# Inverse square roots of the second group's norms computed on DVE instead of POOL

## The chip, the cores and the metric

The kernel runs on one core of a Trainium2 chip. The metric is the device time of one execution in microseconds (us), the median of several runs. In the text, PE is the matrix engine (TensorE), PEld its weight loads, DVE the vector engine, ACT the scalar engine, POOL GpSimd and SP the engine that issues most DMAs.

## The reference, cut to what matters

A block of layers maps `x` (512 tokens of 1024 numbers) to an output of the same shape: a Mamba-2 mixer, a sliding-window attention, a hybrid mixer (gated delta rule and mLSTM), a cross-attention to a memory of 256 tokens, and a feed-forward layer that picks 128 of 16384 experts per token (PEER). Between them stand RMS norms, and these are what the change touches:

```python
def rmsnorm(x, w):
    xf = x.astype(jnp.float32)
    y = xf * lax.rsqrt(jnp.mean(xf * xf, axis=-1, keepdims=True) + EPS)
    return (y * w.astype(jnp.float32)).astype(x.dtype)
```

Every layer norms its input; the Mamba and attention layers also norm their output (`post_norm`) and, inside, the gated outputs; the hybrid layer norms each head (128 numbers) separately; a final norm ends the kernel. In each case one number per token (or one per token and head) goes through `1/sqrt(mean + EPS)`.

## The kernel before, in words

The 512 tokens are four blocks of 128, each block on the 128 partitions. Two **groups** of two blocks go through the layers one after the other: `run` iterates over `GROUPS`, and for each group `layers` runs `mamba`, `swa`, `hybrid`, `cross` and `route`. The last group ends in `dense`, which multiplies by all 16384 experts instead of gathering some.

The first group's experts are fetched by **gathers**: 512 indirect DMAs on POOL's queue (`Rows.next`, L1955), each of 128 rows of 4 KB, and for each a **gather product** on DVE of 128x1024 elements (`Rows.take`, L1989 with the table `p_u`, L1995 with `p_v`). These run as side work while the second group goes through its layers: `after` is a generator that `run` advances by a share at each `yield` of `layers`. It first finishes the first group's routing, then sets `self.rows = Rows(...)` (L1928; until then `self.rows` is None) and places the gathers. `self.quiet` is a flag that stops `run` from advancing it, set by the last part of each output projection (`out_part`) and by the hybrid's `finish`, cleared at the end of the next `norm_T`. What is left of the gathers by the time of `dense` is placed there, in `steps`.

The order of the instructions on each engine is fixed when the program is built: a list scheduler takes, among the instructions that are ready in its own model, the one of highest priority, which is the program's order raised by `high_priority(HP)` in `norm_T` and `post` and lowered for the side work. Inside `manual_schedule` (in `dense`) the order is the one written. On the chip each engine runs its queue strictly in this order.

`rstd` (L457) makes the inverse square roots. `v = ss * scale + EPS` is one DVE instruction (L460), then one POOL instruction raises `v` to the power -0.5 (L462), reading a constant tile `mhalf`. Its callers are

- `norm_T` (L499, tile `nr`, 128x1): the sums of squares of a block, then `xn = x * r` in two DVE instructions (L502), then PE transposes (L414) of both blocks, eight ACT copies (L512) into `hh`, and the first matmuls of the next layer;
- `post` (L613, tile `pr`, 128x1), at the end of `mamba` and `swa`, once for each block, with the residual update L618 behind it;
- `mamba` (L851, tile `gr`, 128x2), the gate norm, read later by `post` (L612, L615);
- `finish` in `hybrid` (L1380, tile `or`, 128x4), four times for a group: both blocks for the mLSTM heads, then both for the delta-rule heads. L1378 and L1379 scale the sums before it, L1382 and L1383 apply the result, and a POOL instruction (L1381) multiplies by the gate;
- `final` (L1866, tile `finr`, 128x1), once for each block of the kernel, between an ACT square with its sum (L1865) and the DVE product L1871 with the weights that a DMA brings (`gu<-in_bcw`, L1869); then the output DMA (L1872). For the first group's two blocks `final` is a side work of `Rows` (`ends`), for the second group's it is the end of `dense`.

The weights come as DMAs on SP's queue; ACT and DVE split the unrounded ones into a high and a low part (L378, L381).

Of the kernel before, what the change touches and what calls it, by code (L numbers as in the profile page):

```python
# [9 lines left out]
F32 = mybir.dt.float32  # L10
F32R = mybir.dt.float32r
BF16 = mybir.dt.bfloat16
I32 = mybir.dt.int32
U32 = mybir.dt.uint32
AF = mybir.ActivationFunctionType
ALU = mybir.AluOpType
# [171 lines left out]
class Kern:  # L188
# [268 lines left out]
    def rstd(self, ss, n, name, scale):  # L457
        nc = self.nc
        v = self.pp.tile([128, n], F32, name=name + "v", tag="rsv", bufs=2)
        nc.vector.tensor_scalar(v, ss, scale, EPS, op0=ALU.mult, op1=ALU.add)  # L460
        r = self.pp.tile([128, n], F32, name=name + "r", tag="rsr", bufs=3)
        nc.gpsimd.tensor_tensor(r, v, self.mhalf[:, :n], op=ALU.pow)  # L462
        return r

    def hT_open(self, gt, halo, full):
        nc = self.nc
        hx = [self.hp.tile([128, 8, gt + 4], F32 if full else F32R, name=n, tag=n) for n in ("hh", "hl")[:1 if full else 2]]
        if full:
            hx.append(None)
        if halo is not None and full:  # L470
            nc.gpsimd.tensor_tensor(hx[0][:, :, 0:4], *[h.bitcast(F32) for h in halo[0]], op=ALU.add)
        elif halo is not None:
            for j in range(2):
                if halo[0] is None:
                    nc.vector.tensor_copy(hx[j][:, :, 0:4], self.zero[:, None, :].to_broadcast([128, 8, 4]))
                else:
                    nc.gpsimd.tensor_copy(hx[j][:, :, 0:4], halo[0][j])
        self.hx = hx
        self.hT_cur = [t if t is None else t[:, :, 4:] for t in hx]
        return self.hT_cur  # L480
# [1598 lines left out]
```

## Time and profile before

| what | value |
|---|---|
| median of 3 runs | 2506.41 us (2500.04 to 2513.98) |
| the profiled execution | 2507.27 us |
| its span, first to last instruction | 2505.5 us |
| PE busy | 2346.4 us, 94% of the span |
| DVE busy | 1975.4 us, 79% |
| ACT busy | 1177.5 us, 47% |
| POOL busy | 1075.9 us, 43% |
| mean granted clock of PE | 0.97 |

How to read it: a share of busy time is a mean over stages with different limits, and PE's counts pipelined matmuls. The second group's layers run from about 800 us to about 1600 us of the span, `dense` from there to the end. In a timeline row stand the start, the busy time, engine, line, operation, output and inputs, the shape, how many instructions were merged, and in brackets the engine's idle time before it with what released it.

### The profile page before, as it was taken

To read this page: it belongs to the slowest core of one execution; us is meant where nothing else is said; L and a number is where in the kernel's file an instruction comes from. 1 tells how busy PE (TensorE), PEld (TensorE's weight loads), DVE (VectorE), ACT (ScalarE), POOL (GpSimd) and SP (SyncE) were. 2 spreads that over 40 slices of the span, in tenths; PEclk is the share of its full clock that TensorE was granted. 3 is DMA by queue.
4 is the path that set the end of the run, shared out by engine and by line. 5 is a ranking of instruction groups with operands and counts; after the bars stand their busy time and mean duration, and the time that the engine had idled before them with its cause. 6 is when DMAs were issued, how large, how long until landed. Compare 5 with 4: busy or idle time off the path is not lost.

```text
span 2505.5 us, 40945 instructions
## 1 busy us (share of the span) xinstructions
PE 2346.4 (94%) x14872; PEld 2117.7 (85%) x14872; DVE 1975.4 (79%) x3978; ACT 1177.5 (47%) x2451; POOL 1075.9 (43%) x910
## 2 busy tenths in 40 slices
PE   7999998999988999989899968999999999999997
PEld 7999898998888888877778857888999999888864
DVE  7777666757579888877789775799888988888886
ACT  6766566744554433424343222226754454444433
POOL 1111101232010577764648664322246666666663
PEclk9999999999999999999989989999999999999999
DMA  6554434423545799977988768877989999899985
GB/s 205 180 173 158 163 98 142 130 93 103 172 136 166 287 379 363 377 275 277 358 326 297 258 197 329 282 241 239 302 290 355 347 366 360 321 357 344 340 295 176
DMA packets 203961, 642.32 MB, mean 256 GB/s; under 512 B 21104, under 2 KB 53360, under 8 KB 202480
## 3 DMA queue, kind: packets, MB, share of 16 engines
q1 hardware_dynamic: 97216, 347.19, 39.9%
q0 software_dynamic: 73728, 268.47, 29.6%
q10 hardware_dynamic: 32816, 24.06, 3.0%
q8 instruction: 117, 1.92, 0.3%
q14 instruction: 84, 0.69, 0.1%
HBM read 621.74 MB, written 17.89 MB: 255 GB/s over the span
## 4 chain that ended last, share of the span: by engine, by line
PE 63%; DVE 14%; DMA 8%; issue 7%; POOL 4%; ACT 4%; ACTq 0%; DVEq 0%; POOLq 0%; SPq 0%
PE mm L406 41%; PE ax L406 16%; DMA gu<-in_p_v,eid 4%; PE tp L414 3%; DVE wlo L381 3%; PE tp L406 3%; DVE x L1995 2%; POOL gu L1955 1%; DVE cacc L535 1%; ACT whi L378 1%; DMA gd<-gst 1%; DVE act L1811 1%; DMA ol<-in_p_v,eid 0%; DVE xn L502 0%; DVE wk L1531 0%
## 5 line engine op out<-in xcount | busy, mean ns | idle before, releaser
L381 DVE TENSOR_TENSOR wlo<-wraw,whi 128x1024 fp32r<-128x1024 f32 x285 | 353.0, 1244 | 124.0 <-ACT whi L378 122.0
L406 PE MATMUL mm<-hl,whi 128*128 128x256 f32 (+1 forms) x1376 | 391.8, 285 | 0.0
L378 ACT CAST whi<-wraw 128x1024 fp32r<-128x1024 f32 x285 | 298.0, 1050 | 125.8 <-PE mm L406 82.0
L1955 POOL DMA_INDIRECT gu<-in_p_u,eid x190 | 250.2, 1317 | 245.7 <-DVE gu L1989 162.0
L406 PE MATMUL mm<-hh,whi 128*128 128x260 f32 (+1 forms) x1232 | 331.5, 343 | 2.7 <-DVE spp L566 1.5
L1955 POOL DMA_INDIRECT gu<-in_p_v,eid x206 | 297.5, 1444 | 68.8 <-issue 33.1
L406 PE MATMUL mm<-hh,wlo 128*128 128x260 f32 (+1 forms) x1200 | 321.7, 340 | 4.0 <-DVE wlo L381 4.0
L1995 DVE SCALAR_TENSOR_TENSOR x<-gu,act,x 128x1024 f32<-128x1024 f32 x206 | 272.3, 1322 | 48.4 <-DMA gu<-in_p_v,eid 45.2
L406 PEld LDWEIGHTS mm<-hl,whi 128*128 128x128 f32 x1376 | 262.6, 191 | 5.0
L406 PEld LDWEIGHTS mm<-hh,whi 128*128 128x128 f32 x1232 | 235.2, 194 | 21.6 <-ACT hh L512 2.8
L1989 DVE SCALAR_TENSOR_TENSOR gu<-gu,hf 128x1024 f32<-128x1024 f32 x190 | 239.4, 1274 | 17.0 <-DMA gu<-in_p_u,eid 14.5
L406 PEld LDWEIGHTS mm<-hh,wlo 128*128 128x128 f32 x1200 | 231.7, 196 | 20.6 <-DVE wlo L381 4.8
L1818 POOL TENSOR_TENSOR w<-act,w 128x256 fp32r<-128x256 f32 x128 | 146.5, 1144 | 211.9 <-issue 158.7
L406 PE MATMUL mm<-dhh,wlo 128*128 128x256 f32 x752 | 211.6, 281 | 0.0
L406 PE MATMUL mm<-dhh,whi 128*128 128x256 f32 x752 | 209.8, 279 | 0.0
L1813 ACT CAST w<-act 128x256 fp32r<-128x256 f32 x128 | 52.2, 408 | 326.0 <-DVE act L1811 326.0
L406 PE MATMUL mm<-wlo,hh 128*128 128x256 f32 x656 | 175.5, 328 | 0.0
L406 PE MATMUL mm<-whi,hh 128*128 128x256 f32 x608 | 166.8, 328 | 0.4 <-ACT hh L512 0.4
L406 PE MATMUL mm<-whi,oh 128*128 128x256 f32 x560 | 147.0, 326 | 0.0
L406 PE MATMUL mm<-hh,wraw 128*128 128x256 f32 (+1 forms) x608 | 145.4, 385 | 0.4 <-ACT act L1713 0.4
L406 PEld LDWEIGHTS mm<-dhh,whi 128*128 128x128 f32 x752 | 141.1, 188 | 4.0
L406 PEld LDWEIGHTS mm<-dhh,wlo 128*128 128x128 f32 x752 | 141.2, 188 | 0.0
(504 smaller groups left out, 5913.6 us busy)
## 6 DMA issues: line engine op xcount, KB each, us to landing
wraw<-in_w SPq DMA_DIRECT2D x238, 512.0 KB
wraw<-in_p_v SPq DMA_DIRECT2D x78, 512.0 KB
wraw<-in_p_ut SPq DMA_DIRECT2D x69, 512.0 KB
whi<-in_w SPq DMA_DIRECT2D x55, 512.0 KB
wlo<-in_w SPq DMA_DIRECT2D x55, 512.0 KB
wrawd<-in_p_v SPq DMA_DIRECT2D x50, 512.0 KB
wrawd<-in_p_ut SPq DMA_DIRECT2D x36, 512.0 KB
gd<-gst ACTq DMA_DIRECT2D x32, 384.0 KB
```

What stands on the lines that cost most here:

```text
L378: nc.scalar.copy(hi, raw)
L381: (nc.gpsimd if le == "P" else nc.vector).tensor_tensor(lo, raw, hi.bitcast(F32), op=ALU.subtract)
L406: inst = self.last = self.nc.tensor.matmul(out, lhsT, rhs, start=start, stop=stop, skip_group_check=True)
L414: return self.nc.tensor.transpose(out, in_, self.ident[:in_.shape[0], :in_.shape[0]])
L535: nc.vector.scalar_tensor_tensor(acc, ps[:, 1 + j:1 + j + gt], w[:, j:j + 1], acc, op0=ALU.mult, op1=ALU.add)
L1811: nc.vector.tensor_tensor(act, act, G[:, e // 16 % 2, :, e % 16], op=ALU.mult)
L1813: nc.scalar.copy(wt[:, 0:gt], act)
L1818: nc.gpsimd.tensor_tensor(wt[:, gt:2 * gt], act, wt[:, 0:gt].bitcast(F32), op=ALU.subtract)
L1955: self.behind(k.nc.gpsimd.indirect_dma_start(out=t, out_offset=None, in_=table, in_offset=bass.IndirectOffsetOnAxis(ap=self.res[b][0][:, s ...
L1989: self.behind(nc.vector.scalar_tensor_tensor(t, t, 1.0, self.hf[:, b, :], op0=ALU.mult, op1=ALU.mult, accum_out=acts[b][:, s:s + 1]))
L1995: self.behind(nc.vector.scalar_tensor_tensor(x[:, b, :], t, acts[b][:, s:s + 1], x[:, b, :], op0=ALU.mult, op1=ALU.add))
```

## The change

`rstd` calls a new function `pow`. While `self.rows` is None it issues the POOL instruction as before. Later it issues 14 DVE instructions: the bits of `v` as an integer are shifted right by one and subtracted from a constant, which gives a first guess, and three Newton steps of four instructions each refine it, every instruction reading the result of an earlier one. One more small tile (`rst`) is allocated. Nothing else is changed.

```diff
@@ -459,8 +459,24 @@
         v = self.pp.tile([128, n], F32, name=name + "v", tag="rsv", bufs=2)
         nc.vector.tensor_scalar(v, ss, scale, EPS, op0=ALU.mult, op1=ALU.add)
         r = self.pp.tile([128, n], F32, name=name + "r", tag="rsr", bufs=3)
-        nc.gpsimd.tensor_tensor(r, v, self.mhalf[:, :n], op=ALU.pow)
+        self.pow(r, v, n)
         return r
+
+    def pow(self, r, v, n):
+
+        nc = self.nc
+        if self.rows is None:
+            nc.gpsimd.tensor_tensor(r, v, self.mhalf[:, :n], op=ALU.pow)
+            return
+        t = self.pp.tile([128, n], F32, name="rst", tag="rst", bufs=2)
+        ri = r.bitcast(I32)
+        nc.vector.tensor_scalar(ri, v.bitcast(I32), 1, None, op0=ALU.logical_shift_right)
+        nc.vector.tensor_scalar(ri, ri, -1.0, 1597463007.0, op0=ALU.mult, op1=ALU.add)
+        for _ in range(3):
+            nc.vector.tensor_tensor(t, r, r, op=ALU.mult)
+            nc.vector.tensor_tensor(t, t, v, op=ALU.mult)
+            nc.vector.tensor_scalar(t, t, -0.5, 1.5, op0=ALU.mult, op1=ALU.add)
+            nc.vector.tensor_tensor(r, r, t, op=ALU.mult)
```

## Rows read from the trace of the kernel before

**Rows 1.** Page, chain of waits that ended last: shares of the span by engine.
```profile
PE 63%; DVE 14%; DMA 8%; issue 7%; POOL 4%; ACT 4%; ACTq 0%; DVEq 0%; POOLq 0%; SPq 0%
```

**Rows 2.** Line L462, 800 to 1600 us: ns min/median/max, first and last start.
```profile
L462 POOL TENSOR_TENSOR nr<-nv,mhalf x8: 545/554/579, 1098.7 to 1590.2; 128x1 f32<-128x1 f32 x8
L462 POOL TENSOR_TENSOR pr<-pv,mhalf x4: 544/561/573, 1089.9 to 1246.9; 128x1 f32<-128x1 f32 x4
```

**Rows 3.** Timeline, Mamba's end to the attention's norm.
```profile
1097.50 0.19 ACT L493 ACTIVATION_READ_ACCUMULATOR xn<-x 128x1 f32 x1
...
1099.26 0.88 DVE L502 TENSOR_SCALAR xn<-x,nr 128x512 f32<-128x512 f32 x2 [1.94 <-POOL nr L462]
...
1100.06 0.15 DVE L495 TENSOR_TENSOR ns<-nss 128x1 f32<-128x1 f32 x1
1100.24 0.15 DVE L460 TENSOR_SCALAR nv<-ns 128x1 f32<-128x1 f32 x1
1100.48 0.55 POOL L462 TENSOR_TENSOR nr<-nv,mhalf 128x1 f32<-128x1 f32 x1 [1.25 <-DVE nv L460]
1101.06 0.88 DVE L502 TENSOR_SCALAR xn<-x,nr 128x512 f32<-128x512 f32 x2 [0.66 <-POOL nr L462]
```

**Rows 4.** Timeline, first and last of six dependent DVE instructions (rope angles).
```profile
1102.48 0.17 DVE L881 TENSOR_SCALAR rk<-ang 128x16 f32<-128x16 f32 x1
...
1103.52 0.18 DVE L885 TENSOR_SCALAR ang<-ang 128x16 f32<-128x16 f32 x1
```

**Rows 5.** Groups by line and shape, DVE: count, busy us, mean ns.
```profile
L876 DVE MEMSET inv<- 128x1 f32 x16 | 0.3, 59 | 0.0
```

**Rows 6.** Timeline, the attention's end to the hybrid's norm, second block.
```profile
1249.48 0.19 ACT L493 ACTIVATION_READ_ACCUMULATOR xn<-x 128x1 f32 x1
...
1250.75 0.16 DVE L495 TENSOR_TENSOR ns<-nss 128x1 f32<-128x1 f32 x1
```

**Rows 7.** Timeline, the hybrid's end to the cross-attention's norm, both blocks.
```profile
1505.39 0.27 DVE L460 TENSOR_SCALAR nv<-ns 128x1 f32<-128x1 f32 x2
1508.47 0.94 POOL L1955 DMA_INDIRECT gu<-in_p_u,eid  x1 [5.67 <-DMA out<-gu]
...
1510.05 1.68 DVE L502 TENSOR_SCALAR xn<-x,nr 128x512 f32<-128x512 f32 x4 [4.39 <-POOL nr L462]
```

**Rows 8.** Timeline, the routing's norm, second block.
```profile
1590.82 0.88 DVE L502 TENSOR_SCALAR xn<-x,nr 128x512 f32<-128x512 f32 x2 [0.73 <-POOL nr L462]
```

**Rows 9.** Timeline, the hybrid's head norms.
```profile
1458.66 1.47 DVE L1379 TENSOR_TENSOR so<-so,cf 128x4 f32<-128x4 f32 x1
...
1460.12 1.27 DVE L1995 SCALAR_TENSOR_TENSOR x<-hl,act,x 128x1024 f32<-128x1024 f32 x1
...
1461.32 0.16 DVE L460 TENSOR_SCALAR ov<-so 128x4 f32<-128x4 f32 x1
...
1462.27 2.80 POOL L1381 TENSOR_TENSOR mixed<-mixed,hgate 128x512 f32<-128x512 f32 x2
...
1467.31 0.16 DVE L1382 TENSOR_TENSOR cf<-cf,or 128x4 f32<-128x4 f32 x1 [2.85 <-POOL or L462]
...
1468.31 0.29 PEld L414 LDWEIGHTS tp<-ident,mixed 128*128 128x128 f32 x2 [13.13 <-DVE mixed L1383]
```

**Rows 10.** Timeline, dense stage, the final norm of the first group's second block.
```profile
2473.88 0.15 DVE L460 TENSOR_SCALAR finv<-fss 128x1 f32<-128x1 f32 x1 [1.60 <-ACT gu L1865]
...
2474.82 1.23 DVE L381 TENSOR_TENSOR wlod<-wraw,whid 128x1024 fp32r<-128x1024 f32 x1 [0.78 <-ACT whid L378]
...
2477.25 1.71 DVE L1871 SCALAR_TENSOR_TENSOR gu<-x,finr,gu 128x1024 f32<-128x1024 f32 x1 [0.70 <-DMA gu<-in_bcw]
```

**Rows 11.** Timeline, the end of the kernel.
```profile
2495.46 0.15 DVE L460 TENSOR_SCALAR finv<-fss 128x1 f32<-128x1 f32 x1
...
2496.66 0.15 DVE L460 TENSOR_SCALAR finv<-fss 128x1 f32<-128x1 f32 x1 [1.04 <-ACT gu L1865]
...
2499.80 1.28 DVE L1871 SCALAR_TENSOR_TENSOR gu<-x,finr,gu 128x1024 f32<-128x1024 f32 x1 [0.42 <-DMA gu<-in_bcw]
```

## The prediction

> **What bounds the kernel.** I read the chain of waits first: PE makes up 63% of it, POOL 4% [rows 1]. So PE sets the time, and the change matters only where PE stands still for a norm. Then I read the line of the POOL power instruction, which shows how often it runs in the second group and that one takes 0.55 us [rows 2]. Last I read the timeline around each of them. The reader is to see the same picture at each layer's end: PE is out of work, and a string of short instructions on DVE, POOL and ACT runs with nothing beside it. What is added to this string is added to the time.
>
> **What changes sides.** `self.rows` is set early in the second group's Mamba layer, after its input norm; so that norm stays on POOL, and 21 calls change: 1 `gr`, 4 `pr`, 8 `nr`, 4 `or`, 4 `finr`. POOL loses 21 instructions, DVE gains 21 x 14 = 294. No DMA moves; no tile of any size is added.
>
> **The price of one chain.** Today, from the start of `nv` on DVE to the start of `xn`, which reads POOL's result, it takes 1101.06 - 1100.24 = 0.82 us [rows 3]. After the change 14 dependent DVE instructions lie between. The trace has none on integers, so I bound the step by the nearest rows. Below: independent 128x1 memsets take 0.06 us each [rows 5]. Above: six dependent instructions on 128x16 start over 1.04 us, five steps of 0.21 us [rows 4]. Nearest is the pair of dependent 128x1 instructions, 0.18 us [rows 3]; I take 0.19. Then `nv` to `xn` takes 15 x 0.19 = 2.85 us, and one **passage** costs 2.85 - 0.82 = +2.0 us (bounds: 15 x 0.06 - 0.82 = +0.1 and 15 x 0.21 - 0.82 = +2.3). Two chains whose inputs are ready together can share these 2.85 us, since an instruction of the other chain fits into each gap. [...]
>
> **Part by part.**
> 1. `gr`: 0. Its reader comes at the layer's end, behind the other output columns; without that cover, one passage, +2.0.
> 2. Mamba to attention: +1.7. On the path lie the second block's `pr` and then its `nr`, two passages, +4.0. Something comes back: the sum of squares for the second `nr` was there at 1097.50 + 0.19 = 1097.7, but DVE took it up only at 1100.06, since in its queue it stands behind the first block's `xn`, which had waited 1.94 us for POOL [rows 3]. The first block's chain can run beside the second's `pr` chain and be done by then: -2.3. If it can't, the gain falls away: +4.0. The first block's `pr` is hidden while PE still works on the second block's columns.
> 3. Attention to hybrid: +2.9. Again two passages, +4.0, and the second block's sum waited from 1249.67 to 1250.75 [rows 6], -1.1. Without that gain +4.0.
> 4. Hybrid's head norms (`or`): -1.0. PE stands 13.13 us for them [rows 9]. The first block's value went from 1461.32 to 1467.31, 6.0 us, mostly in POOL's queue behind other work. A chain of 15 steps of 0.2 us would be done at 1464.3, -3.0. But DVE instructions with two inputs get stuck while POOL multiplies: L1379, 128x4, took 1.47 us where 0.15 is usual. If the chain is held until L1381 ends, 1462.27 + 2.80 = 1465.1, it is done at 1468.1, +0.8. The second block gains the 2.85 us that DVE idled before L1382. I take -1.0, between the two, because the second block ends the wait; bounds -5.9 (-3.0 and the whole 2.85) and +5.1 (four gather products of 1.27 us in the gaps, rival A). The other two `or` come while PE works on the first half of the projection: 0. [...]
> 5. Final norm of the first group's first block: 0. It is side work; if it delays the output DMA, it delays the gather that waited for that DMA [rows 7] by at most one passage, +2.0.
> 6. Hybrid to cross: -1.7. Both `nv` are ready at 1505.39, but POOL's queue stood behind a gather that waited 5.67 us for an output DMA, so `xn` started at 1510.05 [rows 7]. Two chains side by side end at about 1505.5 + 2.85 = 1508.3. One after the other, with 0.84 us of `xn` between, the second `xn` starts at 1505.5 + 2 x 2.85 + 0.84 = 1512.0 instead of 1510.9: +1.1.
> 7. Cross to routing: +2.0, one passage, of the second block [rows 8]; the first block's runs while PE finishes.
> 8. Final norm in the dense stage: +1.2. The order there is as written, so 14 instructions stand in front of the split L381: it starts at 2473.88 + 2.85 = 2476.7, not 2474.82. L1871 stands behind L381, so it starts at 2476.7 + 1.23 = 2477.9 at the earliest, not at 2477.25 (+0.7), and at most the whole shift of L381 later (+1.9) [rows 10]; I take the middle. ACT queues behind its output DMA, and PE behind ACT. Bounds 0 (PE has slack there) and 1.9.
> 9. The last two final norms: +1.0. The weights' DMA hides much: the last product starts at 2499.80 [rows 11]. With the chains side by side the second ends at 2496.66 + 2.85 = 2499.5, and if the first product stands in its middle, the last starts at about 2500.8. One chain after the other: 2495.46 + 2.85 + 1.28 + 2.85 = 2502.4, +2.6.
>
> Sum: 0 + 1.7 + 2.9 - 1.0 + 0 - 1.7 + 2.0 + 1.2 + 1.0 = +6.1 us. The profiled execution took 2507.27 us, so 2513.4; it lies 0.9 above the median of the runs, so I give **2512.5 us**. About 0.5%, 12.5 us, is what a measurement of this kernel can tell from no change; the forecast is no change.
>
> **Rivals.**
> A. *Gather products in the gaps of the chains* (slower). The order is fixed at build time, and a step that isn't ready lets lower work pass. The trace shows it: between L1379 and L460, which needs it, stands a product of 1.27 us [rows 9]. A 14-step chain has 14 such gaps. Place: the `or` chains, in part `gr` and the side work's final norm. Each product on the path costs 1.27 us; it decides from five on (6.1 + 6.4 = 12.5). With ten, +18.8: 2525 us. For it: rows 9. Against it: at the four layer ends `quiet` keeps new products out.
> B. *Short steps* (faster). If dependent steps start as quickly as the memsets, 0.06 us, a passage costs +0.1 instead of +2.0: parts 2 and 3 become -2.1 and -0.9, part 4 -5, part 6 -3.7, part 7 +0.1, parts 8 and 9 0. Sum -11.6: 2495 us, at the edge of faster. Against it: every dependent pair I read takes 0.18 us or more. [...]
> C. *POOL's queue is worth more* (faster). POOL's queue is in order, so a power instruction that waits for DVE also holds the gathers behind it. Both waits of the head norms would go, 6.0 + 2.85 = 8.9 us [rows 9] instead of 1.0: the sum falls to -1.8. Each gather product that DVE, with its data there earlier, can do ahead of PE's wait instead of in it gives 1.27 us more; it decides from nine on (-13.2). With eight, -12: 2495 us. Against it: in rows 7 the gather waits for a DMA, not for a power.
> D. *It doesn't do what it says*: the words speak of places without gather products, the guard tests only whether `rows` is set. If order and waits stay as they are and the chains hide, about 2507.
>
> **Chances.** Forecast 0.60, A 0.20, B 0.07, C 0.08, D 0.05. The forecast's own range, from its bounds, is 2503 to 2521. Slower by over 0.5%: most of A and little of the forecast's upper end, 0.19. Faster: about half of B and of C and the forecast's lowest end, 0.11. Same: 0.70. The range 2498 to 2524 leaves out the upper half of A and the lower ends of B and C.
>
> **What would show it.** Right: `nv` to `xn` about 2.85 us in the attention's, hybrid's and routing's norms, PE's wait there 2 to 3 us longer; before the cross-attention `xn` about 2 us earlier; L381 in rows 10 about 2 us later. Wrong: products of 1.27 us between the Newton steps, steps well under 0.15 us, or a shift in the dense stage before its last 30 us, where the change touches nothing.

## The result, and the profile after

The changed kernel takes **2521.84 us** (median of 7 runs, 2514.64 to 2526.12) against 2506.41 us before: ratio 1.0068, 95% interval 1.0047 to 1.0088. On another chip it was 1.0055 (1.0036 to 1.0074). So it is slower by 14 to 15 us, where the forecast was +6.1. The time lies in the forecast's range (2498 to 2524), but there by luck: it is above the forecast's own range (2503 to 2521) and inside the wider one only because that had been stretched for rival A. And the sign that had most of the chance, "no change", did not come: both values are just over the 0.5% that the text named, and the intervals reach to both sides of it.

| | before | after |
|---|---|---|
| the profiled execution, its span | 2507.27, 2505.5 us | 2526.12, 2524.3 us |
| PE busy | 2346.4 us, 94% | 2350.0 us, 93% |
| DVE busy | 1975.4 us, 79% | 2009.3 us, 80% |
| POOL busy | 1075.9 us, 43% | 1049.0 us, 42% |
| mean granted clock of PE | 0.970 | 0.965 |

The page of the changed kernel, first its busy times, then the engines' shares of the chain that ended last:

```profile
PE 2350.0 (93%) x14872; PEld 2121.2 (84%) x14872; DVE 2009.3 (80%) x4272; ACT 1177.7 (47%) x2451; POOL 1049.0 (42%) x889
```

```profile
PE 70%; DVE 14%; DMA 5%; issue 4%; ACT 4%; POOL 3%; ACTq 0%; DVEq 0%; POOLq 0%; SPq 0%
```

DVE has 294 instructions and 33.9 us more, POOL 21 instructions less, as told. The chain [rows 1] shows no new bound: PE leads, DVE's share is the same 14%, POOL gives one point. The page can't show where 15 us went. For that the same PE instruction is looked up in both timelines, and the difference of its start is followed along the kernel. Where it jumps, time was lost.

| place (part of the forecast) | forecast | changed | changed, second profile |
|---|---|---|---|
| Mamba to attention (2) | +1.7 | +5.8 | +5.8 |
| attention to hybrid (3) | +2.9 | +4.1 | +5.8 |
| head norms (4) | -1.0 | +0.3 | +0.5 |
| hybrid to cross (6) | -1.7 | -2.3 | -2.6 |
| cross to routing (7) | +2.0 | +3.0 | +3.0 |
| dense stage's final norm (8) | +1.2 | +0.6 | +0.6 |
| last two final norms (9) | +1.0 | +2.4 | +2.4 |
| sum | +6.1 | +13.9 | +15.5 |

The second profile is that of experiment 10, the same kernel. The row of the dense stage ends at the first `finv` of the last two norms, and the row behind it is the time from there to the last product (L1871, after the change L1887). The sums fit the medians (15.4 and 14.3 us) within 1.6. How far such a jump can be read: up to 1050 us the change touches nothing, and there all but two of the thirteen other profiles lie between -3.3 and +3.0 us of before, those two at -7.0 and +6.0. A jump is taken over 20 to 50 us, so this drops out. Shifts outside the table do not go with the change: between 1285 and 1300 us nine of the thirteen profiles, with the change and without, are 1.4 us faster there than before; and in the dense stage up to 2470 us the two profiles of the changed kernel drift by +2.6 and +1.5, the others by -5.0 to +3.8.

PE's clock is in the jumps too: behind Mamba, behind the attention and at the cross-attention PE goes on at a granted clock of 0.50 after its standstill, and the clock is back 4.2 to 8.8 us later; how many differs from profile to profile. The start of the second block's first transpose (L414), the first matmul that needs its `xn`, shows each place almost without that. There the changed kernel's two profiles have +4.6 and +4.5 behind Mamba, +5.0 and +6.8 behind the attention, -1.5 and -1.5 at the cross-attention, +2.7 and +2.7 at the routing. What the clock adds to the jumps (+1.3, -0.9 or -1.0, -0.8 or -1.1, +0.3) nearly cancels, so the loss is that of the chains. The +6.8 holds 1.6 us that are not theirs: in the second profile the first block's `pv` is already that much late.

Below the diff all lines are 16 higher than before. A Newton step is L476 to L479. The line of the last of its four instructions, for `nr`: duration in ns, minimum, median and maximum:

```profile
L479 DVE TENSOR_TENSOR nr<-nr,rst x24: 152/159/233, 1104.5 to 1604.4; 128x1 f32<-128x1 f32 x24
```

One takes 0.16 us, and where nothing else is on DVE the next starts 0.19 us after it, as the forecast took it from [rows 3, 4]. The price of a step was right; what was wrong is how many of these chains stand alone, and what else is on their path.

**The cross-attention's norm** came out as told. Timeline of the changed kernel, to compare with [rows 7]:

```profile
1518.99 0.27 DVE L460 TENSOR_SCALAR nv<-ns 128x1 f32<-128x1 f32 x2
...
1521.68 0.28 DVE L479 TENSOR_TENSOR nr<-nr,rst 128x1 f32<-128x1 f32 x2
1521.87 1.67 DVE L518 TENSOR_SCALAR xn<-x,nr 128x512 f32<-128x512 f32 x4
...
1522.50 1.39 PE L414 MATMUL tp<-ident,xn 128*128 128x128 f32 x4 [4.97 <-DVE xn L518]
```

The same PE row of the kernel before:

```profile
1510.68 1.39 PE L414 MATMUL tp<-ident,xn 128*128 128x128 f32 x4 [6.46 <-DVE xn L502]
```

Each DVE row is a pair, one instruction of each block. Both chains together take 2.88 us from `nv` to `xn`, no more than one alone (2.87 us at the routing, below). PE's wait is 1.5 us shorter (4.97 against 6.46), the -1.7 of the forecast; the rest of the -2.3 and -2.6 is PE's clock, which came back 5.4 and 5.1 us after PE went on, 7.4 before.

**The routing's norm**, timeline of the changed kernel [rows 8]:

```profile
1600.74 0.88 DVE L518 TENSOR_SCALAR xn<-x,nr 128x512 f32<-128x512 f32 x2
...
1601.54 0.15 DVE L514 TENSOR_REDUCE ns<-xss 128x1 f32<-128x4 f32 x1
1601.72 0.15 DVE L460 TENSOR_SCALAR nv<-ns 128x1 f32<-128x1 f32 x1
...
1604.59 0.88 DVE L518 TENSOR_SCALAR xn<-x,nr 128x512 f32<-128x512 f32 x2
```

The second block's `nv` to `xn` is 2.87 us, the passage of +2.0. But its sum (L514) starts only when the first block's `xn` (L518 at 1600.74) is through, and that comes late too, since the first block's chain was not hidden: PE's first transpose there is 0.75 us late, the second block's 2.75. The last 0.3 of the +3.0 is PE's clock.

**The head norms**, timeline of the changed kernel [rows 9]:

```profile
1473.86 0.15 DVE L460 TENSOR_SCALAR ov<-so 128x4 f32<-128x4 f32 x1
...
1474.02 1.25 DVE L2011 SCALAR_TENSOR_TENSOR x<-ol,act,x 128x1024 f32<-128x1024 f32 x1
...
1474.81 2.80 POOL L1397 TENSOR_TENSOR mixed<-mixed,hgate 128x512 f32<-128x512 f32 x2
1475.19 1.22 DVE L473 TENSOR_SCALAR or<-ov 128x4 int32<-128x4 int32 x1
...
1476.99 0.64 DVE L474 TENSOR_SCALAR or<-or 128x4 int32<-128x4 int32 x1
...
1479.30 1.27 DVE L2011 SCALAR_TENSOR_TENSOR x<-ol,act,x 128x1024 f32<-128x1024 f32 x1
...
1480.64 1.27 DVE L2011 SCALAR_TENSOR_TENSOR x<-gu,act,x 128x1024 f32<-128x1024 f32 x1
...
1483.05 0.17 DVE L1398 TENSOR_TENSOR cf<-cf,or 128x4 f32<-128x4 f32 x1
...
1484.07 0.29 PEld L414 LDWEIGHTS tp<-ident,mixed 128*128 128x128 f32 x2 [16.36 <-DVE mixed L1399]
```

From `ov` to the use of `or` it is 9.2 us (6.0 before): two instructions of the chain get stuck while POOL multiplies (L473 takes 1.22 us and L474 0.64, beside L1397), and three gather products stand in its gaps. The first of them ran there before as well (at 1461.48), but then beside POOL's queue, not in the chain's. This is the place that rival A named, with three products instead of five or more. PE's wait is 3.2 us longer, yet the jump is only +0.3, because the second block's `cf`, which ends the wait, follows 1.3 us behind the first's (at 1484.39), 3.2 us before (at 1470.53, when DVE idled for POOL).

**The dense stage**, timeline of the changed kernel [rows 10]:

```profile
2490.49 0.15 DVE L460 TENSOR_SCALAR finv<-fss 128x1 f32<-128x1 f32 x1 [1.60 <-ACT gu L1881]
...
2493.28 1.23 DVE L381 TENSOR_TENSOR wlod<-wraw,whid 128x1024 fp32r<-128x1024 f32 x1
```

L381 comes 2.79 us after `finv` (0.94 before), as told, and 0.6 us of this reaches the last two norms (the table; 2 and 9, which have this norm on DVE too, show +0.6 as well, the profiles that leave it on POOL -0.1 to +0.3).

**The end**, timeline of the changed kernel [rows 11]:

```profile
2512.67 0.15 DVE L460 TENSOR_SCALAR finv<-fss 128x1 f32<-128x1 f32 x1
...
2513.65 0.18 ACT L1881 ACTIVATION_READ_ACCUMULATOR gu<-x 128x1 f32 x1
...
2515.43 0.15 DVE L460 TENSOR_SCALAR finv<-fss 128x1 f32<-128x1 f32 x1
...
2516.07 1.28 DVE L1887 SCALAR_TENSOR_TENSOR gu<-x,finr,gu 128x1024 f32<-128x1024 f32 x1
...
2519.37 1.29 DVE L1887 SCALAR_TENSOR_TENSOR gu<-x,finr,gu 128x1024 f32<-128x1024 f32 x1
```

The second block's sum is there at 2513.65 + 0.18 = 2513.83, but its `finv` starts at 2515.43, behind the first block's whole chain. That is the serial case, which the forecast had as its bound (+2.6): from the first `finv` to the last product it takes 6.70 us, in the second profile 6.69, and 4.34 before.

### The profile page after: what moved, and what is told of

It reads as the page before. It is cut to its first block, busy times and chain, and to the rows that moved or that the text cites. A ratio compares the mean times of both kernels' runs of the same rounds, so it can differ in the third digit from the quotient of the medians.

```text
span 2524.3 us, 41222 instructions
## 1 busy us (share of the span) xinstructions
PE 2350.0 (93%) x14872; PEld 2121.2 (84%) x14872; DVE 2009.3 (80%) x4272; ACT 1177.7 (47%) x2451; POOL 1049.0 (42%) x889
## 4 chain that ended last, share of the span: by engine, by line
PE 70%; DVE 14%; DMA 5%; issue 4%; ACT 4%; POOL 3%; ACTq 0%; DVEq 0%; POOLq 0%; SPq 0%
PE mm L406 46%; PE ax L406 18%; PE tp L406 3%; PE tp L414 3%; DVE wlo L381 2%; DMA gu<-in_p_v,eid 2%; DMA gd<-gst 1%; DVE cacc L551 1%; ACT whi L378 1%; DMA ol<-in_p_u,eid 1%; DVE gu L2005 1%; POOL gu L1971 1%; DVE x L2011 1%; DVE xn L518 0%; DVE act L1827 0%
## 5 line engine op out<-in xcount | busy, mean ns | idle before, releaser
L381 DVE TENSOR_TENSOR wlo<-wraw,whi 128x1024 fp32r<-128x1024 f32 x285 | 352.0, 1240 | 125.4 <-ACT whi L378 125.3
L1971 POOL DMA_INDIRECT gu<-in_p_u,eid x190 | 243.9, 1284 | 277.5 <-DVE gu L2005 180.8
```

Of the source, the lines that this page charges most:

```text
L381: (nc.gpsimd if le == "P" else nc.vector).tensor_tensor(lo, raw, hi.bitcast(F32), op=ALU.subtract)
L1971: self.behind(k.nc.gpsimd.indirect_dma_start(out=t, out_offset=None, in_=table, in_offset=bass.IndirectOffsetOnAxis(ap=self.res[b][0][:, s ...
```

## The experiments

**Theories.** 1: the Newton chains stand one behind the other on the path at the layer ends, and each of their instructions counts. 2: gather products get into the gaps of the side chains (rival A). 3: another order of transfers or another clock makes the time, not the chains.

They move the 21 calls back to POOL by kind, change the length of the chain, or reorder. Ratios are to the kernel before, on the same chip.

**1. Only `nr` and `pr` on DVE.**

```diff
-        if self.rows is None:
+        if self.rows is None or not (name in ("n", "p")):
```

> Only the input norms (nr) and the norms behind a layer (pr) of the second group go to DVE; gr, the head norms and the final norms stay on POOL. The whole function is computed. Theory 1 (the cost sits in the Newton chains that stand one behind the other at the layer ends): the places measured in the changed kernel's timeline return one by one: Mamba to attention +5.8 us, attention to hybrid +4.1, hybrid to cross -2.2, cross to routing +3.0, sum about +10.7, so about 2517 us. Theory 2 (gather products pulled into the gaps of the long side chains gr, or and fin make the time): at most +3, about 2509. Theory 3 (other order of transfers or another granted clock, not the chains): no relation; the first two places cost much less than 10 together.

2524.28 us, ratio 1.0073 (1.0057 to 1.0089). Jumps: Mamba to attention +5.5, attention to hybrid +6.0 (here too the first `pv` was late, by 1.0), hybrid to cross -2.6, cross to routing +3.1. The whole loss is here, so the gather products in the side chains do not make it; theory 2 falls. 18 us is more than the 11 expected, which is why it was run again (11).

**2. Only `gr`, head norms and final norms on DVE.** (`not (name in ("g", "o", "fin"))` in the same line.)

> The other half: only gr, the head norms and the final norms of the second group go to DVE, nr and pr stay on POOL. The whole function is computed. Theory 1: head norms +0.3, dense stage's final norm +0.6, last two final norms +2.4, sum about +3.3, so about 2510 us, not to be told from no change. Theory 2: about +12, 2518 us, with products of 1.27 us between the steps of gr and or, and PE's wait for the head norms 3 us longer. Theory 3: some few us either way at places where neither chain stands.

2504.45 us, ratio 1.0004 (0.9987 to 1.0021): nothing, theory 2 falls a second time. Head norms +0.3, dense stage +0.6 and the last two final norms +2.4 are there as expected. Mamba to attention has +1.0 although the second block's transpose is not late at all: that is the clock alone (see 9). Against them stands -3.3 at the cross-attention, though its `nr` is on POOL here: see 8.

**3. Only the cross-attention's `nr` on DVE.**

> Only the two norms of the cross-attention's input go to DVE, the one place where the changed kernel was ahead. The whole function is computed. Theory 1: xn starts 2.9 us behind nv instead of 4.66, PE goes on 2.2 us earlier, so about 2504 us; smaller than what the runs can tell apart, but to be seen in the timeline. Theory 2: the same. Rival: the gain in the changed kernel came from another order upstream, then no gain in the timeline here.

2502.06 us, ratio 0.9985 (0.9968 to 1.0001). The jump there is -2.6, of which 1.8 us are PE's shorter wait and the rest is the clock; `nv` to `xn` takes 2.87 us. The gain belongs to this place and needs nothing upstream.

**4. Six Newton steps instead of three.**

```diff
-        for _ in range(3):
+        for _ in range(6):
```

> All as in the changed kernel, but six Newton steps instead of three: 12 more dependent DVE instructions in each chain, 12 x 0.19 = 2.3 us. It computes the same values to more precision. Theory 1: some nine or ten chains stand on the path (two at each of two layer ends, one each at the cross-attention, the routing and the dense stage, one or two at the head norms, two at the end): 9.5 x 2.3 = +22 us over the changed kernel, about 2544. Theory 2: the chains' gaps take in more products of 1.27 us, so over +30. Theory 3: no proportion to the number of steps, under +10.

2542.83 us, ratio 1.0150 (1.0133 to 1.0167), 21 us over the changed kernel (25 over its second time, experiment 10); 22 were expected. The loss grows with the length of the chains. The head norms give +3.6 now, the cross-attention +2.4 instead of -2.3.

**5 and 6. `pr` alone, `nr` alone.**

> Only the four pr of the second group (behind Mamba and attention) go to DVE, all else stays on POOL. The whole function is computed. Theory 1a (the chain of the first block's pr is stretched by evacuations of 0.42 us that DVE takes between its steps, and the second's by the first block's x updates, 0.75 us each; both lie on the path): 4.4 us instead of 0.8 in each, some of it given back by the evacuations that come earlier, so +2.8 to +3.6 us at each of the two layer ends, nothing at the cross-attention and the routing, about +6.5, 2512. Rival 1b, as forecast before (a pr costs 2.85 - 0.82 = 2.0 us, that of the second block alone): +2.0 at each, 2510, with 2.9 us from pv to the x update. Rival 3 (order of transfers): no such steps at the layer ends.

> Only the eight nr of the second group (input norms of attention, hybrid, cross-attention, routing) go to DVE. The whole function is computed. Theory 1a: Mamba to attention +2 to +3 us (the second block's chain 3.9 us with the first block's steps and xn in between, its sum waits 1.0 us instead of 2.36, and the ACT table load of the rope gets ahead of the second evacuation of the norm), attention to hybrid +1.7, hybrid to cross -2.2, cross to routing +3.0, sum about +5, 2511. Together with the kernel with pr alone this gives the loss of the kernel with both. Rival 1b: +1.0, +0.9, -2.2, +2.0, sum +1.7, 2508. Rival 3: no such steps at the layer ends.

`pr` alone: 2510.43 us, ratio 1.0018 (1.0003 to 1.0033), jumps +3.0 and +1.6. `nr` alone: 2510.05 us, ratio 1.0021 (1.0005 to 1.0036), jumps +1.8, +1.2, -2.4 and, at the routing, +3.1. Every place where both kinds stand has a part of each. At the attention's end the kernels that change nothing there (2, 3, 8 and 12) have jumps of -1.3, -0.5, -1.7 and -0.1, although their second block's transposes start within 0.4 us of before. That is PE's clock: it came back 5.8, 7.4, 5.2 and 8.2 us after PE went on, 8.1 in the one profile of before. So the jumps of +1.6 and +1.2 there are too low. Read at the second block's transpose, `pr` alone costs 2.5 behind Mamba and 2.7 behind the attention, `nr` alone 1.7 and 2.2. The sums, 4.2 and 4.8, are what 1 and 11 have with both kinds: 4.2 both times behind Mamba, and behind the attention 5.1 in 11 and 6.4 in 1 with its late `pv`.

**7. Two instructions to a Newton step instead of four.**

```diff
+        nc.vector.tensor_scalar(h, v, -0.5, None, op0=ALU.mult)
...
+                nc.vector.scalar_tensor_tensor(t, r, r, h, op0=ALU.mult, op1=ALU.mult)
...
+            nc.vector.scalar_tensor_tensor(r, t, 1.5, r, op0=ALU.add, op1=ALU.mult)
```

> All 21 calls on DVE as in the changed kernel, same formula, but a Newton step of two dependent instructions instead of four for one column (r*r*h and (t+1.5)*r, with h = -0.5*v off the chain), three for several columns. The chain has 5 or 6 dependent instructions less. Theory 1: 5.5 x 0.19 = 1.0 us less per chain on the path, some 9.5 of them: -10 us against the changed kernel, about 2512, the other half of the line that six steps gave (+22 for 12 instructions). Rival (a fixed cost for each chain moved to DVE, not for each step): under -4 against the changed kernel.

2508.67 us, ratio 1.0014 (0.9997 to 1.0030), 13 us less than the changed kernel and 9 less than its second time (10), which was on the same chip; 10 were expected, under 4 by the rival. Timeline of this kernel, the second block's `pr` behind Mamba:

```profile
1100.64 0.15 DVE L460 TENSOR_SCALAR pv<-pss 128x1 f32<-128x1 f32 x1
...
1101.19 0.22 DVE L479 SCALAR_TENSOR_TENSOR rst<-pr,rsh 128x1 f32<-128x1 f32 x1
1101.45 0.16 DVE L483 SCALAR_TENSOR_TENSOR pr<-rst,pr 128x1 f32<-128x1 f32 x1
...
1102.54 0.21 DVE L635 TENSOR_SCALAR pr<-pr,gr 128x1 f32<-128x1 f32 x1
```

The multiplication with a column as its scalar costs a little more (0.26 us to the next start), but the chain is 1.90 us instead of 2.9. Together with 4 this is nearly a line, some 1.7 to 2.4 us for each dependent instruction of a chain: the loss goes with the number of dependent instructions, not with the move.

**9. As the changed kernel, but the first block's `pr` on POOL.**

```diff
-        if self.rows is None:
+        if self.rows is None or name == "p0":
...
-                r = self.rstd(s1, 1, "p", 1.0 / D)
+                r = self.rstd(s1, 1, "p" if b else "p0", 1.0 / D)
```

> As the changed kernel, but the first block's two pr (behind Mamba and behind attention) stay on POOL; 19 calls are on DVE. The whole function is computed. Theory 1a (the first block's pr is on the path: its chain, stretched to 4.4 us by evacuations, delays the first block's x updates, and these and its last steps stretch the second block's chain from 2.9 to 4.4 us): the second block's pv to its x update 2.9 to 3.1 us, and PE goes on some 2 us earlier than in the changed kernel at each of the two layer ends, sum -4. Rival 1b, as forecast before (the first block's pr is hidden, since PE still works on the second block's columns): no difference at the two layer ends, over 4 us from pv to x update stays.

2516.39 us, ratio 1.0048 (1.0029 to 1.0067). Mamba to attention is still +5.3, only 0.5 less (0.8 at the second block's transpose); attention to hybrid +2.9, 1.2 or 2.8 less (0.9 at the transpose against the first profile). Some 2 were expected at each. So theory 1a, which I had formed from the stretched chain, falls where it was meant to explain most: in the changed kernel the first block's `pr` chain does take 4.40 us, but the evacuations that stand in its gaps are then done earlier, and most of it comes back. This kernel is useful in another way: it is level with before up to there (-0.02 us), so its times can be set beside [rows 3] as they are. Its timeline:

```profile
1094.44 0.15 DVE L460 TENSOR_SCALAR pv<-pss 128x1 f32<-128x1 f32 x1
...
1097.57 1.42 DVE L634 SCALAR_TENSOR_TENSOR x<-ysb,pr,x 128x512 f32<-128x512 f32 x2
...
1099.02 0.16 DVE L511 TENSOR_TENSOR ns<-nss 128x1 f32<-128x1 f32 x1
...
1100.73 0.15 DVE L511 TENSOR_TENSOR ns<-nss 128x1 f32<-128x1 f32 x1
...
1100.92 0.14 DVE L460 TENSOR_SCALAR nv<-ns 128x1 f32<-128x1 f32 x1
...
1102.39 1.08 DVE L518 TENSOR_SCALAR xn<-x,nr 128x512 f32<-128x512 f32 x2
...
1104.84 0.88 DVE L518 TENSOR_SCALAR xn<-x,nr 128x512 f32<-128x512 f32 x2
```

And the one line of the kernel before that answers to the x update:

```profile
1095.52 1.41 DVE L618 SCALAR_TENSOR_TENSOR x<-ysb,pr,x 128x512 f32<-128x512 f32 x2
```

Read down the second block: the x update is 1097.57 - 1095.52 = 2.05 us later, one passage, as forecast. Its sum is taken up at 1100.73 instead of 1100.06, +0.67, so 1.4 us came back (2.3 were forecast). From `nv` to `xn` it is 1104.84 - 1100.92 = 3.92 us instead of 0.82, +3.1 (2.0 were forecast): the first block's chain began at 1099.02, only after the second block's x update in DVE's queue, so its steps and its `xn`, 1.08 us, stand in the middle of the second's chain. 2.05 - 1.4 + 3.1 = +3.8; PE's second transpose is 3.8 us later.

The last 1.5 us are the clock's. Busy time by stretch (start and end, length, then PE, PEld, DVE, ACT, POOL; the third last column is PE's granted clock), first of the kernel before, then of experiment 9, then of experiment 2, where PE went on at 1096.62:

```profile
1092.00:1099.80 7.80, 0.00 (x0) 0.00 (x0) 4.18 (x22) 3.12 (x10) 2.71 (x5) 0.68 0.46 141
1099.80:1104.80 5.00, 3.51 (x12) 2.38 (x13) 4.06 (x16) 2.26 (x5) 2.75 (x3) 0.50 0.39 125
1104.80:1110.00 5.20, 5.20 (x29) 4.58 (x28) 4.20 (x13) 2.65 (x7) 1.36 (x1) 0.98 0.36 120
```

```profile
1092.00:1103.00 11.00, 0.00 (x0) 0.01 (x1) 9.25 (x59) 3.12 (x10) 3.42 (x5) 0.63 0.38 119
1103.00:1108.00 5.00, 2.94 (x10) 1.87 (x11) 2.97 (x19) 2.10 (x3) 0.23 (x1) 0.50 0.60 197
1108.00:1111.00 3.00, 3.00 (x10) 2.35 (x9) 2.02 (x7) 1.07 (x5) 0.00 (x0) 0.50 0.00 0
1111.00:1114.00 3.00, 3.00 (x17) 2.70 (x16) 3.00 (x5) 1.85 (x4) 1.69 (x1) 0.86 0.00 0
```

```profile
1096.60:1101.60 5.00, 3.58 (x13) 2.43 (x14) 4.03 (x16) 2.32 (x5) 2.75 (x3) 0.50 0.44 141
1101.60:1104.60 3.00, 3.00 (x12) 2.39 (x12) 2.04 (x5) 1.86 (x5) 0.00 (x0) 0.64 0.57 182
```

All three times PE goes on at 0.50 after its standstill (7.95 us before, 11.09 in 9, 7.97 in 2). Before, the clock is back some 5 us after PE went on; in 9 PE works at 0.50 for nearly 9 us. Three more microseconds at 0.50 are, as an estimate from these stretches, 1.5 us of work. But the length of the standstill alone does not decide it: in 2 it is that of before, and the clock is back only after 7.1 us, which is its +1.0. In the five profiles whose standstill is that of before or shorter (before, 2, 3, 8, 12) it took 5.2 to 7.1 us, in the changed kernel (twice), 1, 9 and 11, with 11.1 to 12.0 us of standstill, 7.8 to 8.8, and in 4, with 18.3 us, 7.0. So it tends to be later with the change; why stays open.

At the attention's end it went the other way. PE went on at 1250.58 before and at 1265.57 in the changed kernel; in these stretches the clock comes back, before and in the changed kernel:

```profile
1256.00:1260.00 4.00, 4.00 (x17) 3.27 (x16) 3.12 (x3) 1.69 (x4) 3.08 (x4) 0.67 0.68 215
```

```profile
1270.00:1274.00 4.00, 4.00 (x19) 3.10 (x18) 3.89 (x4) 2.08 (x5) 3.32 (x3) 0.77 0.44 135
```

That is some 8.1 us after PE went on before and 6.3 in the changed kernel, so that place's jump has 0.9 us of luck in it.

**10 and 11. The changed kernel, and `nr` with `pr`, once more.** The same code as the changed kernel and as 1.

> The changed kernel itself once more, for a second profile and an interval on this chip. If the steps at the layer ends belong to the kernel, the second profile has them within 0.5 us: Mamba to attention +5.8, cross to routing +3.0, last two final norms +2.4; places where the granted clock or an output DMA decides may differ by 1.4 us: attention to hybrid +4.1 to +5.5, hybrid to cross -2.3, and the 1.5 us inside the attention may be gone. Ratio to before within 1.0047 to 1.0088.

> nr and pr on DVE once more, the rest on POOL. The first time it lost 18 us in the medians, the two kernels with nr alone and pr alone 5.8 and 5.4 together only 11. If the two kinds of chain lengthen each other (pr's end puts nr later, and the rope's table load ahead of the evacuation), the 18 stays and Mamba to attention and attention to hybrid are each longer than the two alone together. If it was the first chip's run, about 2516, 11 us.

The changed kernel: 2518.11 us, ratio 1.0055 (1.0036 to 1.0074). Its second profile has +5.8, +3.0 and +2.4 as expected, and the attention to hybrid at +5.8, a little over the +4.1 to +5.5 expected. A jump of 1.5 us inside the attention, which the first profiles of the changed kernel and of experiment 1 had, is gone; what it was stays open. Theory 3 falls: the places come again, and the clock's parts nearly cancel. `nr` with `pr`: 2517.72 us, ratio 1.0049 (1.0032 to 1.0067), 14 us by the medians and 12 by the ratio, where 5 and 6 together have 11 and 10. Its jumps are +5.3 and +4.7, where 5 and 6 together have +4.9 and +2.8 with the clock in them, and its transposes agree with theirs (see 5 and 6). So the two kinds add up as far as these runs can tell, and the 18 us of the first time were high; the intervals of the two times overlap.

**8 and 12. A version meant to beat both.** All on POOL as before, but the final norm that is side work of the hybrid layer (`fin` of block 0) on DVE, and the attention's memset of `va` with the copy behind it placed after the two input norms on POOL's queue.

```diff
+        if self.rows is None or not (name == "fin0"):
...
-        nc.gpsimd.memset(va, 1.0)
+        m = nc.gpsimd.memset(va, 1.0)
         if gi:
+            self.tc.add_manual_dep(m.ins, self.xn_last.ins.name, mybir.DependencyInfo(
+                mybir.DependencyClass.NoSync, mybir.DependencyReason.SCHED_ONLY), reason="behind the norm")
```

> A version meant to beat both: everything on POOL as before, but the one final norm that is side work of the hybrid layer on DVE, so that POOL's queue has the cross-attention's two nr ahead of the gather that waits for an output DMA; and in the attention POOL's memset and one copy of va are put behind the two input norms. The whole function is computed. Theory 1: in the cross-attention xn starts 0.83 us behind nv instead of 4.66, PE goes on 3.5 us earlier; in the attention the first xn comes 1.15 us earlier, which is 1 us for PE; about -4.5, 2501.5. Rival (what is taken out comes back as a later gather and another wait): no change in the medians, the two places earlier in the timeline but a wait further on longer.

> The version with one final norm on DVE and the memset behind the norms once more, to see whether its gain of 4.8 us holds. Theory 1: 2 to 5 us faster than before again (ratio 0.998 to 0.9992), xn at the cross-attention 0.8 us behind nv. Rival (the gain was the runs' own variation): ratio 0.9995 or more.

2499.84 us, ratio 0.9986 (0.9973 to 0.9999), and the second time 2499.83 us, 0.9981 (0.9968 to 0.9995): 4 to 5 us faster than before, both intervals just below 1, and 18 to 22 faster than the changed kernel. Timeline of 8 at the cross-attention, to compare with [rows 7]:

```profile
1502.25 0.27 DVE L460 TENSOR_SCALAR nv<-ns 128x1 f32<-128x1 f32 x2
1502.54 1.12 POOL L469 TENSOR_TENSOR nr<-nv,mhalf 128x1 f32<-128x1 f32 x2 [0.18 <-DVE nv L460]
1503.14 1.67 DVE L518 TENSOR_SCALAR xn<-x,nr 128x512 f32<-128x512 f32 x4 [0.62 <-POOL nr L469]
...
1503.77 0.41 PE L414 MATMUL tp<-ident,xn 128*128 128x128 f32 x2 [2.97 <-DVE xn L518]
...
1511.93 0.99 POOL L1973 DMA_INDIRECT gu<-in_p_u,eid  x1 [8.27 <-DMA out<-gu]
```

With that one final norm on DVE the build puts the two `nr` ahead of the gather that waits for the output DMA, not behind it, and `xn` starts 0.89 us after `nv`, not 4.66: a jump of -3.3 us (the second time too), more than the change's own gain there. PE's wait is 2.97 us, not 6.46, and the clock came back as late as before (7.4 us after PE went on), so in 8 the -3.3 is all the queue's. In 5 this place has -1.3 with the order and the wait as before:

```profile
1512.73 1.39 PE L414 MATMUL tp<-ident,xn 128*128 128x128 f32 x4 [6.60 <-DVE xn L518]
```

That is the clock, back 4.2 us after PE went on. The move of the memset gave -0.4 and -0.6 at the attention, less than the 1 expected: the first `xn` comes 1 us earlier, but the second takes 1.47 instead of 0.88 us, beside the memset.

## Why the prediction went as it did

The sign of nearly every part was right, the size was not: +6.1 forecast, +13.9 and +15.5 by the timelines. The forecast's own range was too narrow for its working: the upper bounds of its parts 2 to 4 and 6 to 9 (2.0 for part 7) add up to +20.7, 2527, not 2521. Of the signs that it named, `nv` to `xn` in about 2.85 us came at the routing; behind Mamba and the attention the second block took 3.86 and 3.61.

- **The step (0.19 us) and the passage (+2.0)** held: 2.87 us at the routing, 2.88 at the cross-attention, 3.1 from `pv` to the x update in experiment 9, and the line of six, four and two instructions. Rival B is out: its 0.06 us a step is that of the independent memsets [rows 5], and the dependent steps started 0.19 us apart.
- **Part 2** failed in the sentence "The first block's chain can run beside the second's `pr` chain and be done by then: -2.3". It can't: in the queue it stands behind the second block's x update, so the two `nr` chains run into each other and the first `xn` stands in the second. 1.4 us came back, not 2.3, and the second passage was +3.1, not +2.0 (experiment 9). Then 0.8 of the first block's `pr`, which was costed as hidden, and 1.3 to 1.5 us at the lower clock, a term that the sum did not have. Even the bound without the gain, +4.0, was too low, and without the clock too (4.6 and 4.5 at the second block's transpose). **Part 3** is the same picture, mis-sized by 1.2 to 2.9. Its second chain in the changed kernel, 3.61 us, where 0.88 was before:

```profile
1263.47 0.15 DVE L460 TENSOR_SCALAR nv<-ns 128x1 f32<-128x1 f32 x1
...
1267.08 0.88 DVE L518 TENSOR_SCALAR xn<-x,nr 128x512 f32<-128x512 f32 x2
```

- **Part 7** was short by 1.0: "the first block's runs while PE finishes" was wrong, and cost 0.75; the clock added 0.3.
- **Part 9**: the likelier value was the wrong end. The two chains stood one behind the other, +2.4 both times, where the bound was +2.6. **Part 8** was over by 0.6: PE had most of L381's delay to spare.
- **Part 4** (forecast -1.0, measured +0.3 and +0.5) and **part 6** (-1.7, -2.3 and -2.6): part 4 lies within its bounds and holds both halves of its working, the stuck instructions and rival A's products, three of them. Part 6 was right (PE's wait 1.5 us shorter), and its excess is luck of the clock.
- **Part 1** and **part 5** cost nothing that can be seen. Part 5 did something else: it changed the order of POOL's queue at the cross-attention (experiments 2 and 8).

Rival A named the right mechanism, other work in the gaps of a chain, at a place where it cost little. Its price is paid at the layer ends, where `quiet` keeps gather products out, by the other block's steps and `xn`; the three products in `or` cost hardly anything at the end (+0.3), and `or`, `gr` and the final norms together do not move the median (experiment 2). Rival C shows in a small way: POOL's queue was worth something at one place, but by its order, and with the power left on POOL.

## What to carry to other kernels

The chain of short dependent instructions cost its number of instructions times the start-to-start time of a dependent pair, read from the trace (15 x 0.19 us), and this went to the end time where the big engine stood still for it; two such chains cost no more than one where both inputs were ready together (2.88 us at the cross-attention) and stood one behind the other where they were not (6.70 us at the end, 4.34 before), so look in the queue for what stands ahead of the second. Before a helper is moved to another engine for all its calls, price each call by its place: here the two of the cross-attention and one final norm gained something, the other 18 nothing. And compare two timelines where the big engine resumes, not only further on: PE's clock came back 4.2 to 8.8 us after the standstills told of here, 4.2 to 8.2 where nothing had been changed at the place, and this put up to 1.5 us, either way, into single jumps.

## What was not expected of the hardware

- Instructions with one input were slow beside POOL too: in the changed kernel L473 on 128x4 integers took 1.22 us and L474 0.64 (medians 0.17 and 0.16) while POOL multiplied (L1397, two in 2.80 us from 1474.81). The forecast thought only of those with two inputs.
- A second independent chain on the same queue was free: 30 instructions from `nv` to `xn` in 2.88 us, where 15 take 2.87.
- After its standstill behind Mamba PE's clock stayed at 0.50 for 5.2 us in the kernel before and for 8.8 us in experiment 9, with the same matmuls ahead of the standstill; and for 7.1 us in experiment 2, where the standstill too was that of before.
